# Five and seven raw weight buffers, and gate products with both weight halves in 32 columns

## The chip, the core and the metric

The kernel runs on one core of a Trainium2 chip. The metric is device time in microseconds for one execution. Its engines are TensorE (PE, with its weight loads PEld), VectorE (DVE), ScalarE (ACT), GpSimd (POOL) and SyncE (SP), which here only issues transfers. Each runs its own list of instructions in order; TensorE may load weights for the next product during the present one. On-chip tiles live in named rings of buffers ("tags"): asking for a tile of a tag gives the oldest buffer, and the first write to it waits until its last reader is done.

## The reference

Two layers over 256 context and 256 latent tokens of width 1024: a bidirectional mLSTM, then a latent attention, each followed by a gated feed-forward block with a short convolution. What the change touches is the gate computation of the mLSTM and, beyond that, only how weights are brought in.

```python
x_m = h @ w_up
x_c = jax.nn.silu(_dwconv(x_m, conv_w, conv_b))
...
gates = jnp.einsum("bti,zig->zbgt", x_c, w_gates) + b_gates[:, None, :, None]
li = gates[:, :, :M_HEADS].astype(jnp.float32)
lf = jax.nn.log_sigmoid(gates[:, :, M_HEADS:].astype(jnp.float32))
```

There are two directions z, and in each 4 input gates and 4 forget gates (8 columns g) for every token t; the sum over i has 2048 terms. The gates feed cumulative sums and maxima over the tokens, which weight the mLSTM's attention-like products.

## The kernel before, in words

**Split precision.** Every operand of a large product is held as a high part h, rounded to the product's format, and a low part l = x - h. `mm3` (L311 to L315) forms a product of two such operands from three: h times h, h times l, l times h. The terms low times low are left out.

**The weight stream** (`Stream`, L222 to L282). All weights are packed on the host in one array `ws` of tiles of 128 x 1024 floats (512 KB), in the order of use that `_plan` writes out. For each tile, `_load` issues a transfer on SyncE into a buffer of the tag `raw`, of which there are NRAW = 3. `_split` then casts the raw tile to its high part on ScalarE (L257) and subtracts on VectorE for the low part (L258), into a weight slot of the tag `w` (NB = 3) or, for tiles marked wide, into two buffers of the tag `u` (NU = 31, shared with the activations). A raw buffer is free after the subtraction; after each split, `_split` issues loads until NRAW tiles beyond it are under way. `use(key)` first lets splits run up to AHEAD = 8 tiles further, as far as `limit` and the slots allow. `pump` does the same up to a given tile. Wide tiles are those of the tails of the output products `mout`, `fout0`, `aout` and `fout1`, the attention's first weights (`ukn`, `uv`), and the first four of `fin1`.

**Order of the stages.** `start_up` and `w_up` (up projection and convolution), `w_og` and `w_v` (products of 128-token tiles with moving weights of 512 columns), `gates`, then four heads h of `w_qk`, each of four products j of two weight tiles, with the work of earlier heads in between; then the output product `mout` with its layer norm, the feed-forward products `fin0` and `fout0`, the attention (`dkv`, `ukn`, `uv`, `dq`, `uqr`, `uqn`, scores, `aout`), `fin1`, `fout1` and the last layer norm. In each output product (`outmm`) the last few tiles are held (the tail), so that the first token tile t = 0 finishes all its sums before t = 1 starts. Behind it follow the layer norm's rows (`ln_rows`, L943), the transposes with modulation (`ln_T`, L1003) and the next stage's products. For the layer norm behind `aout`, `build` places the splits of the first `fin1` tiles between the two token tiles' rows: up to QA = 2 before, QB = 4 between, QC = 6 after.

**Work in the background.** Generators are advanced by `tick`: each step runs to the next `yield`. The list `bg` holds such work as the gate chain and the heads' weighting, and `bg2` the modulation weights (`ada_all`, L482), which pass through buffers `ar` (2, loads from `ada_w` on SyncE) and accumulators `acc` (2) on VectorE. The tag `ar` also holds the rotary tables (`rope_load`, L1238), read in the attention before the scores. In the four `w_qk` products of a head, each of the eight weight tiles is followed by two steps of `bg`. The order that stands on each engine at the end is made by a scheduler when the kernel is built, from this order of emission and modelled costs; only the start-up's order is written by hand.

**The gates** (`gates`, L680). The gate weights, 16 columns, are spread on the host over 128 columns: input gates of the two directions at columns 0 and 32, forget gates at 64 and 96. Two weight tiles of 8 blocks hold them; for each of 16 blocks k `mm3` issues three products with 512 moving columns (the activations `xc`, all tokens), 48 in all, into one bank. So the sums come out at partitions 0, 32, 64 and 96, where `gate_chain` (L690) reads them: biases on ScalarE, the logarithm of the sigmoid, scans over tokens on VectorE forwards in partitions 0 to 31 and backwards in 32 to 63, an exponential, two small stores of the result `ad` (read by `head` as broadcasts), and eight transposes into `gcol` (L724 to L730).

Of the kernel before, what the change touches and what calls it, by code (L numbers as in the profile page):

```python
# [7 lines left out]
F32 = mybir.dt.float32  # L8
F32R = mybir.dt.float32r
I32 = mybir.dt.int32  # L10
AF = mybir.ActivationFunctionType
ALU = mybir.AluOpType
AX = mybir.AxisListType

D = 1024
# [14 lines left out]
CW = 1024  # L30

NB, NRAW, NU = 3, 3, 31
# [35 lines left out]
def _plan():  # L68
    ids, order = {}, []

    def add(key, cols, wide=False):
        if key not in ids:
            ids[key] = (len(ids), cols)
        order.append((key, wide))
# [6 lines left out]
    for s in range(4):  # L81
        for c in range(8):
            add(("v", s, c), 1024)
    for c in range(2):
        add(("gates", 0, c), 1024)
    for h in range(H0):
# [35 lines left out]
def _pack(i):  # L122
    ids, _ = _plan()
    ws = np.zeros((len(ids), 128, CW), np.float32)
    wg = i["m_w_gates"][0]
    gz = np.zeros((2 * D, 128), np.float32)
    for z in range(2):
        gz[:, 32 * z:32 * z + 4] = wg[z][:, :4]
        gz[:, 64 + 32 * z:64 + 32 * z + 4] = wg[z][:, 4:]
    ukv = i["a_w_ukv"][0].reshape(256, H1, DN + DV)  # L130
# [8 lines left out]
    for key, (n, cols) in ids.items():  # L139
        kind, a, c = key  # L140
# [4 lines left out]
        elif kind == "gates":  # L145
            b = _stat(gz, 0, 8 * c, 8)
        elif kind == "v":
# [74 lines left out]
class Stream:  # L222


    def __init__(self, k, ids, order, ws):
# [5 lines left out]
        self.raw, self.hl = {}, {}  # L231

    def skip(self, n):
        self.nl = self.ns = self.nu = n

    def _load(self):
        k, j = self.k, self.nl
        n, cols = self.ids[self.order[j][0]]
        t = k.pool.tile([128, CW], F32, tag="raw", name="raw", bufs=NRAW)
        k.nc.sync.dma_start(t[:, :cols], self.ws[n, :, :cols])  # L240
        self.raw[j] = t
        self.nl += 1

    def _split(self):
# [8 lines left out]
        else:  # L253
            w = k.pool.tile([128, 2, CW], F32R, tag="w", name="w", bufs=NB)
            h, l = w[:, 0], w[:, 1]
            self.live.append(j)
        k.nc.scalar.copy(h[:, :cols], raw[:, :cols])  # L257
        k.nc.vector.tensor_sub(l[:, :cols], raw[:, :cols], h[:, :cols])  # L258
        self.hl[j] = (h, l)
        self.ns += 1  # L260
        while self.nl < min(self.ns + NRAW, self.n):
            self._load()
# [22 lines left out]
class K:  # L285
# [393 lines left out]

    def gates(self):  # L680
        gp = self.ps("gates")
        for c in range(2):
            w = self.st.use(("gates", 0, c))
            for kk in range(8):
                k = 8 * c + kk
                cs = slice(kk * 128, (kk + 1) * 128)
                self.mm3(gp, (w[0][:, cs], w[1][:, cs]), (self.xc[k][:, 0], self.xc[k][:, 1]), k == 0, k == 15)
        return gp

    def gate_chain(self, gp):  # L690
        nc = self.nc
        bg = self.smc("bg")
        zi, zf, ab = self.s2("zi"), self.s2("zf"), self.s2("ab")
        R = slice(0, 64)
        nc.scalar.activation(zi[R], gp[0:64], AF.Identity, bias=bg[0:64, 0:1], scale=1.0)
        nc.scalar.activation(zf[R], gp[64:128], AF.Identity, bias=bg[64:128, 0:1], scale=1.0)
# [8 lines left out]
        def scan(o, x, op):  # L705
            nc.vector.tensor_tensor_scan(o[0:32], on[0:32], x[0:32], 0.0, op0=ALU.mult, op1=op)
            nc.vector.tensor_tensor_scan(o[32:64, 0:256][:, ::-1], on[32:64, 0:256], x[32:64, 0:256][:, ::-1],
                                         0.0, op0=ALU.mult, op1=op)
            nc.vector.tensor_tensor_scan(o[32:64, 256:512][:, ::-1], on[32:64, 0:256], x[32:64, 256:512][:, ::-1],
                                         o[32:64, 0:1], op0=ALU.mult, op1=op)  # L710
        scan(B, zf, ALU.add)
        nc.vector.tensor_sub(zi[R], zi[R], B[R])
        yield
        scan(ab, zi, ALU.max)
        nc.vector.tensor_add(B[R], B[R], ab[R])
# [875 lines left out]
```

## Time and profile before

| | us |
|---|---|
| median of 3 runs | 1431.02 |
| lowest and highest run | 1429.1 and 1434.94 |
| the profiled execution | 1429.89 |
| its span (first to last instruction) | 1428.1 |

| engine | busy us | share of the span |
|---|---|---|
| TensorE, products | 1398.6 | 98% |
| TensorE, weight loads | 1176.5 | 82% |
| VectorE | 980.5 | 69% |
| ScalarE | 642.3 | 45% |
| GpSimd | 100.1 | 7% |

The mean granted TensorE clock is 0.996 of full. A row of groups or of the timeline names the line, the engine, the operation, what is written and what is read (out<-in, by the program's names without buffer numbers), and the shape; a bracket at the end of a timeline row gives the engine's idle time before it and what ended it. A wait is written as: who waits, for whom, total us, times, longest. In the chain of waits each piece has a start, a length and a name, and is what set the end at that time. Times count from the span's start.

### The profile page before, as it was taken

How to read it: one execution, taken by the hardware profiler on the slowest of the kernel's cores; microseconds unless marked ns; L12 is line 12 of the kernel's file. 1: busy time of each engine (PE TensorE's matmuls, PEld its weight loads, DVE VectorE, ACT ScalarE, POOL GpSimd, SP SyncE). 2: the span in 40 equal slices, each digit the busy share in tenths (PEclk: the TensorE clock that was granted, in tenths of full speed). 3: DMA queues.
4: the chain of work that ended last, by engine and by line, in shares of the span. 5: the costliest groups of instructions: out<-in, count | busy, mean ns of one | idle time of the engine just before them, and what ended most of it. 6: DMA issues, size and time to landing. Idle time of an engine off the chain costs nothing.

```text
span 1428.1 us, 18819 instructions
## 1 busy us (share of the span) xinstructions
PE 1398.6 (98%) x7095; PEld 1176.5 (82%) x7095; DVE 980.5 (69%) x1437; ACT 642.3 (45%) x972; POOL 100.1 (7%) x185
## 2 busy tenths in 40 slices
PE   7999999999999999999999999999999999899997
PEld 3788888888888888888888888888887998899986
DVE  6696778885775666666787444444567888777755
ACT  6554231224334254464553333334364665555542
POOL 0010110003001010210001000000000001000000
PEclk9999999999999999999999999999999999999999
DMA  9475776777774745555635333335666315367763
GB/s 335 172 240 185 238 250 220 253 232 269 252 230 154 221 136 173 178 178 179 207 129 193 91 116 116 121 123 171 191 187 208 122 53 183 124 187 216 223 198 102
DMA packets 82827, 262.70 MB, mean 184 GB/s; under 512 B 11352, under 2 KB 19752, under 8 KB 82736
## 3 DMA queue, kind: packets, MB, share of 16 engines
q1 hardware_dynamic: 68304, 214.82, 48.2%
q0 software_dynamic: 14144, 46.17, 9.6%
q8 instruction: 55, 0.90, 0.3%
q10 hardware_dynamic: 288, 0.52, 0.1%
q14 instruction: 36, 0.29, 0.1%
HBM read 243.56 MB, written 17.91 MB: 183 GB/s over the span
## 4 chain that ended last, share of the span: by engine, by line
PE 65%; issue 18%; DMA 6%; DVE 6%; ACT 3%; POOL 2%; SPq 0%; DVEq 0%; POOLq 0%; ACTq 0%
PE fin L315 8%; PE fin L313 8%; PE fin L314 8%; PE y L314 5%; PE y L315 5%; PE y L313 5%; PE qk L315 4%; PE qk L313 4%; PE qk L314 4%; DMA raw<-in_ws 3%; DMA ar<-in_ada_w 2%; DVE wu L258 1%; PE up L313 1%; DMA xcr<-xcd 1%; PE up L315 1%
## 5 line engine op out<-in xcount | busy, mean ns | idle before, releaser
L258 DVE TENSOR_TENSOR w<-raw,w 128x1024 fp32r<-128x1024 f32 (+2 forms) x267 | 323.9, 1213 | 240.2 <-ACT w L257 239.7
L257 ACT CAST w<-raw 128x1024 fp32r<-128x1024 f32 (+2 forms) x267 | 278.6, 1045 | 437.2 <-PE tok L315 153.3
L315 PE MATMUL fin<-h,w 128*128 128x256 f32 (+1 forms) x696 | 231.6, 333 | 0.5 <-DVE w L258 0.5
L314 PE MATMUL fin<-h,w 128*128 128x256 f32 (+1 forms) x696 | 231.8, 333 | 0.0
L313 PE MATMUL fin<-h,w 128*128 128x256 f32 (+1 forms) x696 | 231.7, 334 | 0.0
L440 DVE SCALAR_TENSOR_TENSOR acc<-ar,cond,acc 128x1024 f32<-128x1024 f32 x112 | 140.6, 1279 | 36.0 <-DMA ar<-in_ada_w 35.6
L315 PEld LDWEIGHTS fin<-h,w 128*128 128x128 f32 x696 | 132.2, 190 | 13.8 <-DVE w L258 0.9
L314 PEld LDWEIGHTS fin<-h,w 128*128 128x128 f32 x696 | 132.2, 190 | 13.0 <-DVE h L1024 0.2
L313 PEld LDWEIGHTS fin<-h,w 128*128 128x128 f32 x696 | 132.0, 190 | 12.8
L313 PE MATMUL qk<-xc,w 128*128 128x512 f32 x256 | 101.1, 395 | 0.0
L313 PE MATMUL tok<-w,xm 128*128 128x512 f32 x256 | 100.4, 392 | 0.0
L315 PE MATMUL qk<-xc,w 128*128 128x512 f32 x256 | 100.1, 391 | 0.2 <-DVE w L258 0.2
L314 PE MATMUL qk<-xc,w 128*128 128x512 f32 x256 | 99.9, 390 | 0.0
L315 PE MATMUL tok<-w,xm 128*128 128x512 f32 x256 | 99.7, 389 | 0.0
L314 PE MATMUL tok<-w,xm 128*128 128x512 f32 x256 | 99.6, 389 | 0.0
L313 PE MATMUL y<-w,act 128*128 128x512 f32 (+1 forms) x212 | 80.4, 379 | 0.0
L315 PE MATMUL y<-w,act 128*128 128x512 f32 (+1 forms) x212 | 80.1, 378 | 0.0
L314 PE MATMUL y<-w,act 128*128 128x512 f32 (+1 forms) x212 | 80.1, 378 | 0.0
L258 DVE TENSOR_TENSOR wu<-raw,wu 128x1024 fp32r<-128x1024 f32 x36 | 43.9, 1222 | 21.7 <-ACT wu L257 21.3
L315 PEld LDWEIGHTS qk<-xc,w 128*128 128x128 f32 x256 | 48.1, 188 | 10.6 <-DVE w L258 0.6
L313 PEld LDWEIGHTS tok<-w,xm 128*128 128x128 f32 x256 | 48.0, 188 | 10.3
L315 PEld LDWEIGHTS tok<-w,xm 128*128 128x128 f32 x256 | 48.1, 188 | 10.1
(357 smaller groups left out, 2756.6 us busy)
## 6 DMA issues: line engine op xcount, KB each, us to landing
raw<-in_ws SPq DMA_DIRECT2D x300, 512.0 KB, 3.9
ar<-in_ada_w SPq DMA_DIRECT2D x80, 512.0 KB, 4.5
adaw<-in_ada_w SPq DMA_DIRECT2D x32, 256.0 KB, 6.5
xcd<-cv POOLq DMA_DIRECT2D x16, 256.0 KB, 3.2
od<-o POOLq DMA_DIRECT2D x16, 256.0 KB, 4.0
vd<-v POOLq DMA_DIRECT2D x16, 256.0 KB, 3.9
xcr<-xcd POOLq DMA_DIRECT2D x16, 256.0 KB, 6.7
vr<-vd POOLq DMA_DIRECT2D x16, 256.0 KB, 3.8
```

Source lines behind the costliest of these rows:

```text
L257: k.nc.scalar.copy(h[:, :cols], raw[:, :cols])
L258: k.nc.vector.tensor_sub(l[:, :cols], raw[:, :cols], h[:, :cols])
L313: mm(out, w[0], x[0], start=start, stop=False)
L314: mm(out, w[0], x[1], start=False, stop=False)
L315: mm(out, w[1], x[0], start=False, stop=stop)
L440: nc.vector.scalar_tensor_tensor(acc[j], w, s, acc[j], op0=ALU.mult, op1=ALU.add)
```

## The change

It has three parts.

1. **Raw buffers.** The ring into which raw weight tiles are loaded is 3 buffers up to the first tile of `fout0`, then 5 (the two `acc` buffers join), and from the first tile of `aout` on 7 (the two `ar` buffers join as well). After a split, loads are issued as far ahead as the ring has buffers.
2. **Gate products.** The gates' weights are packed as 16 columns a block, 256 columns in all, in one tile of 128 KB instead of two of 512 KB. Their high and low parts are written side by side, 32 columns a block. For each of the 16 blocks two products are issued (with the high and with the low part of the activations), 32 in all, into 32 partitions of a bank. The terms low times low are now among them.
3. **Placing.** `gate_chain` builds a 32 x 128 matrix `sel` from the identity, which adds the high and low columns' sums and puts them at the partitions where they were before; splits the 32 rows of sums into a high and a low part; and after three yields issues two products with `sel`. What follows reads the new bank. The scans yield after each direction, so the chain has 14 yields before its transposes, against 8.

```diff
--- before.py
+++ after.py
@@ -81,8 +81,7 @@
     for s in range(4):
         for c in range(8):
             add(("v", s, c), 1024)
-    for c in range(2):
-        add(("gates", 0, c), 1024)
+    add(("gates", 0, 0), 256)
     for h in range(H0):
         for j in range(4):
             for c in range(2):
@@ -122,11 +121,7 @@
 def _pack(i):
     ids, _ = _plan()
     ws = np.zeros((len(ids), 128, CW), np.float32)
-    wg = i["m_w_gates"][0]
-    gz = np.zeros((2 * D, 128), np.float32)
-    for z in range(2):
-        gz[:, 32 * z:32 * z + 4] = wg[z][:, :4]
-        gz[:, 64 + 32 * z:64 + 32 * z + 4] = wg[z][:, 4:]
+    gz = np.concatenate([i["m_w_gates"][0, 0], i["m_w_gates"][0, 1]], axis=1)
     ukv = i["a_w_ukv"][0].reshape(256, H1, DN + DV)
     uq = i["a_w_uq"][0].reshape(384, H1, DN + DR)
     ukn = np.ascontiguousarray(ukv[:, :, :DN]).reshape(256, H1 * DN)
@@ -143,7 +138,7 @@
         elif kind == "og":
             b = _mov(i["m_w_og"][0][:, a * 512:(a + 1) * 512], 2 * c, 2)
         elif kind == "gates":
-            b = _stat(gz, 0, 8 * c, 8)
+            b = gz.reshape(16, 128, 16).transpose(1, 0, 2).reshape(128, 256)
         elif kind == "v":
             b = _mov(i["m_w_v"][0][:, a * 512:(a + 1) * 512], 2 * c, 2)
         elif kind == "qk":
@@ -230,13 +225,23 @@
         self.limit = self.n
         self.raw, self.hl = {}, {}
 
+        keys = [x[0] for x in order]
+        self.bufs = [(0, [("raw", NRAW)] * NRAW)]
+        self.bufs.append((keys.index(("fout0", 0, 0)), self.bufs[-1][1] + [("acc", 2)] * 2))
+        self.bufs.append((keys.index(("aout", 0, 0)), self.bufs[-1][1] + [("ar", 2)] * 2))
+
+    def ring(self, j):
+        return [x for x in self.bufs if x[0] <= j][-1]
+
     def skip(self, n):
         self.nl = self.ns = self.nu = n
 
     def _load(self):
         k, j = self.k, self.nl
         n, cols = self.ids[self.order[j][0]]
-        t = k.pool.tile([128, CW], F32, tag="raw", name="raw", bufs=NRAW)
+        j0, ring = self.ring(j)
+        tag, bufs = ring[(j - j0) % len(ring)]
+        t = k.pool.tile([128, CW], F32, tag=tag, name="raw", bufs=bufs)
         k.nc.sync.dma_start(t[:, :cols], self.ws[n, :, :cols])
         self.raw[j] = t
         self.nl += 1
@@ -254,11 +259,19 @@
             w = k.pool.tile([128, 2, CW], F32R, tag="w", name="w", bufs=NB)
             h, l = w[:, 0], w[:, 1]
             self.live.append(j)
-        k.nc.scalar.copy(h[:, :cols], raw[:, :cols])
-        k.nc.vector.tensor_sub(l[:, :cols], raw[:, :cols], h[:, :cols])
+        src = raw[:, :cols]
+        if key[0] == "gates":
+
+            v = h[:, 0:512].rearrange("p (k x n) -> p k x n", x=2, n=16)
+            src = src.rearrange("p (k n) -> p k n", n=16)
+            k.nc.scalar.copy(v[:, :, 0], src)
+            k.nc.vector.tensor_sub(v[:, :, 1], src, v[:, :, 0])
+        else:
+            k.nc.scalar.copy(h[:, :cols], src)
+            k.nc.vector.tensor_sub(l[:, :cols], src, h[:, :cols])
         self.hl[j] = (h, l)
         self.ns += 1
-        while self.nl < min(self.ns + NRAW, self.n):
+        while self.nl < min(self.ns + len(self.ring(self.ns)[1]), self.n):
             self._load()
 
     def use(self, key, hold=False):
@@ -678,13 +691,13 @@
         self.xm = None
 
     def gates(self):
+
         gp = self.ps("gates")
-        for c in range(2):
-            w = self.st.use(("gates", 0, c))
-            for kk in range(8):
-                k = 8 * c + kk
-                cs = slice(kk * 128, (kk + 1) * 128)
-                self.mm3(gp, (w[0][:, cs], w[1][:, cs]), (self.xc[k][:, 0], self.xc[k][:, 1]), k == 0, k == 15)
+        w = self.st.use(("gates", 0, 0))[0]
+        for k in range(16):
+            for x in range(2):
+                self.nc.tensor.matmul(gp[0:32], w[:, k * 32:(k + 1) * 32], self.xc[k][:, x],
+                                      start=k == 0 and x == 0, stop=k == 15 and x == 1)
         return gp
 
     def gate_chain(self, gp):
@@ -692,6 +705,22 @@
         bg = self.smc("bg")
         zi, zf, ab = self.s2("zi"), self.s2("zf"), self.s2("ab")
         R = slice(0, 64)
+
+        sel = self.pool.tile([32, 128], F32R, tag="s2", name="sel", bufs=13)
+        nc.vector.memset(sel.bitcast(F32), 0.0)
+        for z in range(2):
+            for f in range(2):
+                i = 8 * z + 4 * f
+                nc.vector.tensor_add(sel[:, 64 * f + 32 * z:64 * f + 32 * z + 4], self.ident[0:32, i:i + 4],
+                                     self.ident[0:32, 16 + i:20 + i])
+        g2 = self.u("g2")
+        self.split(g2[0:32, 0], g2[0:32, 1], gp[0:32])
+        yield
+        yield
+        yield
+        gp = self.ps("gates")
+        for x in range(2):
+            nc.tensor.matmul(gp, sel, g2[0:32, x], start=x == 0, stop=x == 1)
         nc.scalar.activation(zi[R], gp[0:64], AF.Identity, bias=bg[0:64, 0:1], scale=1.0)
         nc.scalar.activation(zf[R], gp[64:128], AF.Identity, bias=bg[64:128, 0:1], scale=1.0)
         nc.vector.scalar_tensor_tensor(ab[R], zf[R], -1.0, zf[R], op0=ALU.mult, op1=ALU.max)
@@ -704,14 +733,15 @@
 
         def scan(o, x, op):
             nc.vector.tensor_tensor_scan(o[0:32], on[0:32], x[0:32], 0.0, op0=ALU.mult, op1=op)
+            yield
             nc.vector.tensor_tensor_scan(o[32:64, 0:256][:, ::-1], on[32:64, 0:256], x[32:64, 0:256][:, ::-1],
                                          0.0, op0=ALU.mult, op1=op)
             nc.vector.tensor_tensor_scan(o[32:64, 256:512][:, ::-1], on[32:64, 0:256], x[32:64, 256:512][:, ::-1],
                                          o[32:64, 0:1], op0=ALU.mult, op1=op)
-        scan(B, zf, ALU.add)
+            yield
+        yield from scan(B, zf, ALU.add)
         nc.vector.tensor_sub(zi[R], zi[R], B[R])
-        yield
-        scan(ab, zi, ALU.max)
+        yield from scan(ab, zi, ALU.max)
         nc.vector.tensor_add(B[R], B[R], ab[R])
         nc.vector.tensor_scalar(ab[R], ab[R], -1.0, None, op0=ALU.mult)
         nc.scalar.activation(B[R], B[R], AF.Exp, scale=-1.0)
```

## Prediction

> **What bounds the kernel now.** I read the page first, then the waits of TensorE, then the timeline around each place where it waits.
>
> ```profile
> span 1428.1 us, 18819 instructions
> PE 1398.6 (98%) x7095; PEld 1176.5 (82%) x7095; DVE 980.5 (69%) x1437; ACT 642.3 (45%) x972; POOL 100.1 (7%) x185
> PE zT L1011 <- DVE z L984: 6.1, 2, 5.0
> PE y L314 <- DVE wu L258: 1.2, 2, 0.8
> ACT wu L257 <- DMA raw<-in_ws: 33.0, 26, 3.2
> ```
>
> TensorE is busy 98% of the span, so only two things can pay: fewer products, or the roughly 30 us in which it is not busy. Of the waits (engine, line, awaited instruction: total us, times, longest) the largest outside the start-up is the transposing product behind a layer norm; waits on weights (line 258) are small. ScalarE, however, waits 33.0 us for raw weights that become wide tiles (wu), and those belong to the tails of the output products, which stand right before the layer norms.
>
> **The gate products.** 48 products go; 32 come, and two placing ones. These rows of the timeline are the first gate product and the first product after the last; the chain's row gives 16 modulation products with a stationary of only 4 columns.
>
> ```profile
> 384.19 0.39 PE L313 MATMUL gates<-xc,w 128*128 128x512 f32 x1
> 395.07 0.39 PE L313 MATMUL qk<-xc,w 128*128 128x512 f32 x1
> 46.20 3.70 PE adar L405 x16
> 384.20:395.00 10.80, 10.80 (x49) 8.97 (x48) 5.87 (x6) 2.69 (x4) 1.34 (x3) 1.00 0.94 347
> ```
>
> 48 products take 395.07 - 384.19 = 10.88 us, 0.227 each: the 0.39 us of a record overlaps its neighbours, and the window (length; busy PE, PEld, DVE, ACT, POOL; clock; DMA share; GB/s) is full. A narrow stationary is shown at 3.70/16 = 0.231 us, so narrowness saves nothing per product; only the count does. 34 at 0.231 are 7.85, at 0.227 they are 7.71: the gain is 3.0 to 3.2 us, and I take **3.1**. End to end records (34 x 0.39 = 13.3) would be a loss of 2.4, but the same record length fits 48 in 10.88, which excludes it.
>
> ScalarE and VectorE work changes little: two weight splits of 1024 columns go, one of 256 columns and one of the 32-row sums come, with a memset and four additions of 4 columns. The narrow operations are not in the trace in this form; the nearest are these.
>
> ```profile
> 389.83 1.06 ACT L257 CAST w<-raw 128x1024 fp32r<-128x1024 f32 x1 [3.90 <-PE gates L315]
> 1177.76 0.37 ACT L318 CAST oT<-o 128x256 fp32r<-128x256 f32 x1
> 410.76 0.59 ACT L318 CAST qk<-qk 128x512 fp32r<-128x512 f32 x1
> 415.28 0.69 DVE L319 TENSOR_TENSOR qk<-qk 128x512 fp32r<-128x512 f32 x1
> 396.57 1.22 DVE L258 TENSOR_TENSOR w<-raw,w 128x1024 fp32r<-128x1024 f32 x1
> 421.70 0.18 DVE L465 SCALAR_TENSOR_TENSOR adav<-adav,adab 64x32 f32<-64x32 f32 x1
> ```
>
> ScalarE: 2 x 1.06 out, 0.37 + 0.59 in, a gain of about 1.1. VectorE: 2 x 1.22 = 2.44 out; in come 0.4 (a third of 1.22), 0.69 and five small operations of at most 0.18, together 2.0. Both are even within a microsecond. The stream loses one 512 KB load and shrinks another to 128 KB on SyncE's queue: 0.92 MB, or 2.6 us at 347 GB/s, in a stage whose DMA share is 0.94. That eases the modulation weights which share the queue; I put it at nothing.
>
> The gate chain gets a detour: split of the sums, the two placing products, and only then the biases. It is a new wait: ScalarE's bias waits for the placing product, behind it on ScalarE stand casts of qk weights, and TensorE waits for those. The chain has 8 yields before its transposes now and 14 after, of 16 steps in the first head's qk products (two per half product of 24 x 0.227 = 5.4 us), so the transposes still fit, moved from the fifth half product to the last. How thin the cover is, these rows show.
>
> ```profile
> 407.12 0.63 ACT L698 ACTIVATE ab<-ab 64x512 f32<-64x512 f32 x1 [8.21 <-DVE ab L697]
> 421.04 0.63 ACT L717 ACTIVATE B<-B 64x512 f32<-64x512 f32 x1 [7.45 <-DVE B L715]
> 417.75 0.50 PE L315 MATMUL qk<-xc,w 128*128 128x512 f32 x1 [0.16 <-DVE w L258]
> ```
>
> ScalarE stood 8.21 and 7.45 us behind the chain, yet TensorE lost only 0.16: three weight slots hide it, with nothing to spare at 417.75. With the chain later and cut finer (a scan per step, 1.2 us at most, where three scans and a subtraction stood in one) I price it at nothing, with bounds of +0.16 gained and, if the cover is gone, the 8.21 + 7.45 = 15.7 lost.
>
> **Five raw buffers, from the first fout0 load.** With three, a load waits for the subtraction three tiles back. Loads keep SyncE's order, and a load into a former ada_w buffer waits for that work's last reader; the last modulation reduction starts at 783.7 us (its row: 141.1 to 783.7), well before the fout0 products.
>
> ```profile
> L447 DVE TENSOR_REDUCE adar<-adat x32: 643/672/686, 141.1 to 783.7; 128x16 f32<-128x512 f32 x32
> 1081.42 1.05 ACT L257 CAST wu<-raw 128x1024 fp32r<-128x1024 f32 x1 [1.92 <-DMA raw<-in_ws]
> 1082.12 0.39 PE L313 MATMUL y<-wu,act 128*128 128x512 f32 x1
> 1085.21 0.49 PE L314 MATMUL y<-wu,act 128*128 128x512 f32 x1 [0.45 <-DVE wu L258]
> 1101.43 0.28 PE L313 MATMUL kn<-ckT,wu 128*128 128x256 f32 x1
> 1163.45 0.87 PE PT L1373 x8
> 1102.45 1.21 DVE L258 TENSOR_TENSOR wu<-raw,wu 128x1024 fp32r<-128x1024 f32 x1
> 1106.67 0.98 PE L1011 MATMUL zT<-ident,z 128*128 128x128 f32 x7 [1.04 <-DVE z L984]
> ```
>
> The fout0 tail is 6 tiles x 4 banks x 3 = 72 products. From 1082.12 to 1101.43 it takes 19.3 us where 72 x 0.227 are 16.3; of the 3.0 over, six transposes among them are 0.65 (8 in 0.87, the row of attention). At most 2.3 is then lost to late weights, one wait of 0.45 among it; the loss may also be switching between kinds of products. I take half, **1.2** (bounds 0 and 2.3). The following layer norm holds the transposes for 1.04; a weight subtraction of 1.21 lies inside it that earlier loads would move ahead. I take half, **0.5** (0 to 1.04).
>
> **Seven raw buffers, from the first aout load.** The last two share space with the rotary tables, whose use ends before attention. Here are the aout tail and the layer norm behind it.
>
> ```profile
> 1206.27 1.05 ACT L257 CAST wu<-raw 128x1024 fp32r<-128x1024 f32 x1 [3.25 <-DMA raw<-in_ws]
> 1215.82 1.05 ACT L257 CAST w<-raw 128x1024 fp32r<-128x1024 f32 x1 [2.48 <-DMA raw<-in_ws]
> 1207.37 0.50 PE L313 MATMUL y<-wu,oT 128*128 128x512 f32 x1 [0.69 <-ACT wu L257]
> 1220.82 0.28 PE L315 MATMUL y<-wu,oT 128*128 128x256 f32 x1
> 1222.80 1.23 DVE L258 TENSOR_TENSOR w<-raw,w 128x1024 fp32r<-128x1024 f32 x1
> 1224.28 1.22 DVE L258 TENSOR_TENSOR w<-raw,w 128x1024 fp32r<-128x1024 f32 x1
> 1227.34 2.82 PE L1011 MATMUL zT<-ident,z 128*128 128x128 f32 x12 [5.01 <-DVE z L984]
> 1221.00:1232.00 11.00, 5.64 (x28) 5.07 (x28) 8.95 (x21) 7.52 (x16) 0.00 (x0) 0.69 0.51 166
> ```
>
> The wait of 0.69 goes with its restart: **0.8** (0 to 0.85). Then 1227.34 - 1220.82 = 6.5 us pass between the last output product and the transposes, and VectorE spends 1.23 + 1.22 of it on splits for the next stage, which came late because the casts before them stood 3.25 and 2.48 us waiting for raw weights. With seven tiles loaded during attention these splits can be over before the last product. I take **2.0** of the 2.45 (bounds 0, if the weight slots and not the loads hold them, and 2.45).
>
> The clock in this window is 0.69. [...]
>
> **The end.** These pieces of the chain show what arrives last in fout1.
>
> ```profile
> 1357.67 0.23 PE y L313
> 1360.45 0.23 PE y L313
> 1399.97 4.30 DMA raw<-in_ws
> 1404.35 1.06 ACT wu L257
> 1405.43 1.24 DVE wu L258
> 1419.81 0.13 PE y L315
> ```
>
> The three-tile cycle is 4.30 + 1.06 + 1.24 = 6.6 us, 2.2 a tile, against 1360.45 - 1357.67 = 2.78 us of products a tile. So the loads barely lead, and the last tiles hold the tail up. 22 x 2.78 = 61.2 from 1357.67 ends at 1418.8; it ended at 1419.9. I take **1.0** (0 to 1.1).
>
> **Sum.** 3.1 + 1.2 + 0.5 + 0.8 + 2.0 + 1.0 = 8.6 us. The profiled execution took 1429.89 (1.8 around its span), so 1421.3; the median of the runs is 1.1 above it, which makes **1422.4**. Its own range: all upper bounds are 3.2 + 2.3 + 1.0 + 0.9 + 2.5 + 1.1 = 11.0 (1420), the gate products with half of the rest about 5.9 (1425), and a shift in the order of the engines' work may move either by 2: 1418 to 1427.
>
> **Rivals.** (1) The deeper ring is hidden anyway: wide tiles and weight slots, not raw buffers, set when a split can start, and ScalarE's 33.0 us only change their name. For it: a cast can also wait for TensorE to free a slot (the 3.90 in the gate rows), and TensorE's own wait for wu is 1.2 us in all. Against: the last tile follows exactly by load, cast and subtraction. Then only 3.1 is left: 1427.9, no change.
>
> (2) Slower: the qk stage of the first head loses its cover. The placing products put a TensorE round trip ahead of ScalarE's chain, the casts behind it come late, and the 8.21 and 7.45 land on TensorE. That costs 15.7 - 8.6 = 7.1: 1438.1. It decides from a stall of 8.6 us on. For it: the 0.16 shows no slack. Against: the sums' split is emitted three steps (8 us) ahead of the products that read it.
>
> (3) The gap behind aout gets so short that the clock stays up in it: the 12 transposes take 2.82 us where 8 take 0.87 at full clock, so 1.3, or 1.5 less.
>
> With all other bounds reached, 11.0 + 1.5 = 12.5: 1418.5. For it: 6.5 - 2.45 leaves 4.1 us, some two thirds of what it is. Against: VectorE and ScalarE still have a whole layer norm to do in it. [...]
>
> **How the numbers follow.** The forecast has 0.48, the hidden ring 0.25, the lost cover 0.10, the kept clock 0.17. The range 1415 to 1431 holds the forecast, the hidden ring and the kept clock with an allowance of 3 to 4 us for their sizes. No change means within 0.5%, 7.2 us, about what a measurement of this kernel can tell: 1423.9 to 1438.2. About 0.7 of the forecast lies below it (0.34), nearly all of the kept clock (0.16) and a little of the hidden ring (0.03): faster 0.53. Slower takes most of the lost cover's upper half and a little for other orders: 0.07. The rest, 0.40, is no change.
>
> **What would show it.** The gate and placing products should take about 7.8 us in all, and the first qk product start 3 us earlier; a wait of TensorE on line 258's successor between 395 and 440 us would be the lost cover. ScalarE's wait of 33.0 for raw wide tiles should shrink to a third; if it does and the waits for z and wu stay, the hidden ring is right. The stretch from the last aout product to the transposes should fall from 6.5 to about 4.5. The forecast is wrong if the span shrinks by under 4 or over 13 us.

## The result and the profile after

The changed kernel takes 1422.28 us (median of 6 runs, 1420.65 to 1426.16) against 1430.68 for the kernel before (6 runs, 1429.1 to 1434.94): a ratio of 0.9936 with a 95% interval of 0.9926 to 0.9947. The forecast was 1422.4, worked out from 1431.02, the median of the first three of those six runs.

The page of the kernel after opens with its span and the engines' busy time (us, share of the span, number of instructions).

```profile
span 1418.5 us, 18778 instructions
PE 1392.4 (98%) x7081; PEld 1170.7 (83%) x7081; DVE 979.2 (69%) x1442; ACT 639.2 (45%) x972; POOL 100.1 (7%) x185
```

The span is 9.6 us shorter. Products were busy 1398.6 us and are busy 1392.4: 6.2 less; the other 3.4 are idle time that went. Lines have moved: `mm3` is now L326 to L328, the cast of a split L270, its subtraction L271, the gate products L699, the placing products L723, the transposes behind a layer norm L1041. The view of waits of the kernel after (who waits, for whom: total us, times, longest):

```profile
PE zT L1041 <- DVE z L1014: 2.6, 1, 2.6
...
PE qk L328 <- DVE w L271: 1.2, 1, 1.2
...
ACT wu L270 <- DMA raw<-in_ws: 9.9, 9, 2.8
...
DVE acc L453 <- DMA ar<-in_ada_w: 39.1, 36, 3.5
```

ScalarE's wait for raw wide tiles fell from 33.0 to 9.9. The transposes' wait behind the layer norms fell from 6.1 to 2.6. The second row was 0.16 us in the kernel before: TensorE now waits 1.2 us for a weight split in the first head's qk stage. The last row, VectorE's wait for modulation weights, is needed further down.

The gate products, in the view of one tile (durations in ns as min/median/max, first and last start, shape), and TensorE's timeline of the kernel after (start, us, engine, line, operation, idle time before it in brackets):

```profile
L699 PEld LDWEIGHTS gates<-xc,w x32: 107/108/112, 383.6 to 390.7; 128*32 128x32 f32 x32
L699 PE MATMUL gates<-xc,w x32: 387/392/398, 383.8 to 391.0; 128*32 128x512 f32 x32
L723 PEld LDWEIGHTS gates<-g,sel x2: 181/182/184, 402.2 to 402.3; 32*128 32x128 f32 x2
```

```profile
383.79 7.56 PE L699 MATMUL gates<-xc,w 128*32 128x512 f32 x32
391.19 0.40 PE L326 MATMUL qk<-xc,w 128*128 128x512 f32 x1
...
401.86 0.39 PE L328 MATMUL qk<-xc,w 128*128 128x512 f32 x1
402.18 0.73 PE L723 MATMUL gates<-g,sel 32*128 32x512 f32 x2
402.83 0.50 PE L326 MATMUL qk<-xc,w 128*128 128x512 f32 x1
...
425.31 0.39 PE L327 MATMUL qk<-xc,w 128*128 128x512 f32 x1
426.90 0.50 PE L328 MATMUL qk<-xc,w 128*128 128x512 f32 x1 [1.20 <-DVE w L271]
427.24 0.39 PE L326 MATMUL qk<-xc,w 128*128 128x512 f32 x1
...
1216.05 0.28 PE L328 MATMUL y<-wu,oT 128*128 128x256 f32 x1
...
1219.42 1.72 PE L1041 MATMUL zT<-ident,z 128*128 128x128 f32 x12 [2.65 <-DVE z L1014]
```

32 products take 391.19 - 383.79 = 7.40 us, 0.231 each, although loading a narrow stationary took 108 ns (the first row above). The two placing products put 402.83 - 401.86 = 0.97 us between two neighbours that are otherwise 0.227 apart: 0.74 for both. The stall at 426.90 lengthens the way from 425.31 to 427.24 to 1.93 us, where two products' pitch is 0.45: 1.48 lost. Behind aout, 1219.42 - 1216.05 = 3.4 us pass between the last product and the transposes, from 6.5.

The span can be cut at the starts of products. The table gives the length of each stage that differs, from TensorE's timeline of both kernels.

| stage | before us | after us | gained |
|---|---|---|---|
| start of the span to the first gate product | 384.2 | 383.8 | 0.4 |
| gates: first gate product to first qk product | 10.9 | 7.4 | 3.5 |
| first head's qk: to its first score product | 45.0 | 47.0 | -2.0 |
| fout0 tail: first wide product to first kn product | 19.3 | 18.5 | 0.8 |
| layer norm and kn: to the last kn product | 37.9 | 37.0 | 0.9 |
| aout: first wide to last product | 22.0 | 21.1 | 1.0 |
| gap: to the last wide fin1 product | 21.4 | 18.2 | 3.1 |
| rest of fin1 | 115.3 | 115.1 | 0.2 |
| fout1: first to last product | 62.1 | 60.9 | 1.2 |

The stages between (heads, mout, fin0, most of fout0, attention) differ by at most 0.1. The end behind the last product differs by 0.3. So the gates brought 3.5 and gave 2.0 back one stage later, and the stages that the prediction named for the ring brought 7.2 with the rest of fin1. The 0.8 of the tail is what was left after a new loss: transposes in it now wait 1.23 us for VectorE, where they waited 0.17. TensorE's timeline of the kernel after:

```profile
1083.71 0.44 PE L1221 MATMUL ckT<-ident,ckr 128*128 128x128 f32 x2 [1.23 <-DVE ckr L1173]
```

### The profile page after: what moved, and what is told of

Read it like the earlier page. It is cut to its first block, busy times and chain, and to the rows that moved or that the text cites. A ratio compares the mean times of both kernels' runs of the same rounds, so it can differ in the third digit from the quotient of the medians.

```text
span 1418.5 us, 18778 instructions
## 1 busy us (share of the span) xinstructions
PE 1392.4 (98%) x7081; PEld 1170.7 (83%) x7081; DVE 979.2 (69%) x1442; ACT 639.2 (45%) x972; POOL 100.1 (7%) x185
## 4 chain that ended last, share of the span: by engine, by line
PE 67%; issue 18%; DMA 5%; DVE 5%; ACT 2%; POOL 2%; SPq 0%; DVEq 0%; POOLq 0%; ACTq 0%
PE fin L326 8%; PE fin L328 8%; PE fin L327 8%; PE y L327 6%; PE y L326 6%; PE y L328 6%; PE qk L328 3%; PE qk L326 3%; PE qk L327 3%; DMA ar<-in_ada_w 2%; DMA raw<-in_ws 2%; PE up L326 1%; PE up L328 1%; PE up L327 1%; DMA xcr<-xcd 1%
## 5 line engine op out<-in xcount | busy, mean ns | idle before, releaser
L271 DVE TENSOR_TENSOR w<-raw,w 128x1024 fp32r<-128x1024 f32 (+2 forms) x265 | 321.4, 1213 | 229.3 <-ACT w L270 228.8
L270 ACT CAST w<-raw 128x1024 fp32r<-128x1024 f32 (+2 forms) x265 | 276.8, 1045 | 428.9 <-PE tok L328 136.8
L328 PE MATMUL fin<-h,w 128*128 128x256 f32 (+1 forms) x696 | 231.5, 333 | 0.5 <-DVE w L271 0.5
L326 PE MATMUL fin<-h,w 128*128 128x256 f32 (+1 forms) x696 | 231.7, 334 | 0.0
L453 DVE SCALAR_TENSOR_TENSOR acc<-ar,cond,acc 128x1024 f32<-128x1024 f32 x112 | 140.5, 1279 | 39.6 <-DMA ar<-in_ada_w 39.1
L328 PEld LDWEIGHTS fin<-h,w 128*128 128x128 f32 x696 | 132.2, 190 | 13.7 <-DVE w L271 0.9
L326 PEld LDWEIGHTS fin<-h,w 128*128 128x128 f32 x696 | 132.1, 190 | 13.1
L328 PE MATMUL qk<-xc,w 128*128 128x512 f32 x256 | 100.2, 391 | 1.2 <-DVE w L271 1.2
L326 PE MATMUL qk<-xc,w 128*128 128x512 f32 x256 | 101.1, 395 | 0.0
L326 PE MATMUL tok<-w,xm 128*128 128x512 f32 x256 | 100.4, 392 | 0.0
L328 PE MATMUL tok<-w,xm 128*128 128x512 f32 x256 | 99.7, 389 | 0.0
L326 PE MATMUL y<-w,act 128*128 128x512 f32 (+1 forms) x212 | 80.4, 379 | 0.0
L328 PE MATMUL y<-w,act 128*128 128x512 f32 (+1 forms) x212 | 80.1, 378 | 0.0
L328 PEld LDWEIGHTS qk<-xc,w 128*128 128x128 f32 x256 | 48.0, 188 | 11.9 <-DVE w L271 2.0
L326 PEld LDWEIGHTS qk<-xc,w 128*128 128x128 f32 x256 | 48.1, 188 | 10.4 <-PE gates L723 0.4
L326 PEld LDWEIGHTS tok<-w,xm 128*128 128x128 f32 x256 | 48.0, 188 | 10.4
L328 PEld LDWEIGHTS tok<-w,xm 128*128 128x128 f32 x256 | 48.0, 188 | 10.1
```

Source lines behind the costliest of these rows:

```text
L270: k.nc.scalar.copy(h[:, :cols], src)
L271: k.nc.vector.tensor_sub(l[:, :cols], src, h[:, :cols])
L326: mm(out, w[0], x[0], start=start, stop=False)
L328: mm(out, w[1], x[0], start=False, stop=stop)
L453: nc.vector.scalar_tensor_tensor(acc[j], w, s, acc[j], op0=ALU.mult, op1=ALU.add)
```

## The experiments

Three questions were open: which part of the change brings what; whether seven buffers do more than five; and whether the stall in the first head's qk stage comes from the change. The table puts all runs together; each is compared with runs of the kernel before that were measured beside it. The stage columns come from one profile of each kernel and add two rows of the table above: gates + qk, tail + kn, aout + gap.

| kernel | median us | before us | ratio, 95% interval | gates + qk | tail + kn | aout + gap |
|---|---|---|---|---|---|---|
| before | | | | 55.9 | 57.2 | 43.4 |
| after | 1422.28 | 1430.68 | 0.9936 (0.9926 to 0.9947) | 54.4 | 55.5 | 39.3 |
| gates_only | 1429.97 | 1433.37 | 0.9985 (0.9975 to 0.9995) | 55.6 | 57.7 | 43.5 |
| rings_only | 1423.76 | 1433.37 | 0.9945 (0.9926 to 0.9964) | 56.8 | 54.9 | 39.8 |
| five_only | 1423.67 | 1433.37 | 0.9949 (0.9931 to 0.9966) | 57.1 | 55.2 | 38.4 |
| seven_only | 1427.37 | 1433.37 | 0.9965 (0.9953 to 0.9977) | 59.1 | 57.0 | 38.1 |
| noada_before | 1430.97 | 1432.46 | 0.9986 (0.9975 to 0.9998) | 55.4 | 60.1 | 43.7 |
| noada_gates | 1426.92 | 1432.46 | 0.9954 (0.9935 to 0.9973) | 52.7 | 57.1 | 43.7 |
| warm | 1421.22 | 1432.46 | 0.9918 (0.9903 to 0.9933) | 54.6 | 55.8 | 38.6 |
| after_poolq | 1427.3 | 1432.46 | 0.9960 (0.9947 to 0.9972) | 59.4 | 55.3 | 40.5 |
| late | 1424.96 | 1431.98 | 0.9944 (0.9930 to 0.9957) | 52.5 | 54.9 | 39.5 |
| late_warm | 1424.74 | 1431.98 | 0.9946 (0.9932 to 0.9960) | 52.5 | 55.3 | 38.3 |
| gates_five | 1422.06 | 1431.98 | 0.9929 (0.9914 to 0.9943) | 55.4 | 54.9 | 40.0 |
| changed_again | 1421.7 | 1431.98 | 0.9929 (0.9915 to 0.9943) | 54.6 | 55.5 | 38.6 |

### One part alone: gates_only, rings_only

gates_only is the changed kernel with three raw buffers throughout; rings_only is the kernel before with the changed ring.

```diff
--- after.py
+++ gates_only.py
-        self.bufs.append((keys.index(("fout0", 0, 0)), self.bufs[-1][1] + [("acc", 2)] * 2))
-        self.bufs.append((keys.index(("aout", 0, 0)), self.bufs[-1][1] + [("ar", 2)] * 2))
```

> The gate products and the placing as in the changed kernel, three raw buffers throughout. Theory (the gain of the gate products is partly given back in the first head's qk stage): 1.5 to 2.2 us faster than before, about 1428.6; the stretch from the first qk product to the first score product of head 0 is near 47.0 us as in the changed kernel (45.0 before), with one wait of TensorE of about 1.2 us on a weight subtraction in it; everything after head 0 keeps its length. Rival (the stall is made by the deeper ring or is chance): 3.1 us faster, 1427.5, and the stretch is 45.0 to 45.6 us.

> The gates as before, five and then seven raw buffers. Theory (the two parts act in different stages and add up): 7.3 us faster, about 1423.4, with the gap from the last aout product to the twelve transposes at 3.4 us (6.5 before). Rival (the parts help each other by shifting the schedule): under 5 us faster.

The ring alone gives 0.55% and the gates alone 0.15%; both together gave 0.64% and, in changed_again, 0.71%. The parts add up within their intervals, and most of the gain is the ring. gates_only leaves tail + kn and aout + gap about as they were before (57.7 and 43.5); rings_only has them about as after (54.9 and 39.8). The qk stage of gates_only took 48.2 us, so the stall is there without the deeper ring; its size is taken up below. In rings_only the way from the last aout product to the twelve transposes took 4.4 us, not the 3.4 that was expected.

### Five or seven: five_only, seven_only, gates_five

five_only keeps five buffers from fout0 to the end; seven_only keeps three up to aout and then takes all seven; gates_five is the changed kernel without the third ring.

```diff
--- rings_only.py
+++ five_only.py
-        self.bufs.append((keys.index(("aout", 0, 0)), self.bufs[-1][1] + [("ar", 2)] * 2))
```

```diff
--- rings_only.py
+++ seven_only.py
-        self.bufs.append((keys.index(("fout0", 0, 0)), self.bufs[-1][1] + [("acc", 2)] * 2))
-        self.bufs.append((keys.index(("aout", 0, 0)), self.bufs[-1][1] + [("ar", 2)] * 2))
+        self.bufs.append((keys.index(("aout", 0, 0)), self.bufs[-1][1] + [("acc", 2)] * 2 + [("ar", 2)] * 2))
```

> The gates as before, five raw buffers from the first fout0 tile to the end. If five are enough for the aout and fout1 tails too (a cycle of 4.4 + 1.05 + 1.24 = 6.7 us over five tiles is 1.3 us a tile, below the 2.2 of three and below the products' 2.8): as fast as five and seven, 7 us faster. If the two further buffers carry the aout stage: only the 1.6 us of the fout0 tail and the layer norm behind it, plus 1.1 of fout1, so 2.7 us faster.

> The gates as before, three raw buffers up to the first aout tile, seven from there. If the stages are independent: 7.3 less 1.6, so 5.7 us faster, the fout0 tail and the stretch to the last kn product as long as before (19.3 and 37.9 us). If the gap behind aout depends on how early the weights before aout arrived: under 4 us faster.

> The changed kernel with five raw buffers kept to the end instead of seven. If the two further buffers are not needed: within 0.1% of the changed kernel, the gap behind aout and the fout1 stage as long as there (18.2 and 61.1 us). If they are: 2 us or more slower, with the gap nearer to 21.

five_only takes as long as rings_only, and gates_five as long as changed_again beside it (the same ratio, 0.9929). With five buffers to the end, aout took 21.0 us and fout1 60.9 in both kernels, as with seven (21.1 and 60.9). seven_only has the gain behind aout (38.1) but not the one in tail + kn (57.0). Its TensorE timeline shows the old wait still there behind fout0, and another one of which more is said below:

```profile
421.25 0.50 PE L324 MATMUL qk<-xc,w 128*128 128x512 f32 x1 [2.59 <-DVE w L267]
...
1109.80 0.98 PE L1020 MATMUL zT<-ident,z 128*128 128x128 f32 x7 [1.04 <-DVE z L993]
```

The wait of 1.04 is that of the kernel before, to the hundredth; the timelines of five_only and of the changed kernel have no wait of these transposes there. So buffers 4 and 5 do the whole work and the two that come from the rotary tables add nothing that these runs can tell.

### The stall in the first head's qk stage: noada_before, noada_gates

Up to the start of fin0 the kernels before, rings_only, five_only and seven_only issue the same instructions in the same order on every engine. Still their qk stage took 45.0, 46.0, 46.2 and 48.3 us. What differs is how long TensorE waits for a weight split: 0.16 us in the kernel before, 2.59 in seven_only (the row above). VectorE's timeline of the kernel after shows what the split stands behind:

```profile
399.19 1.28 DVE L453 SCALAR_TENSOR_TENSOR acc<-ar,cond,acc 128x1024 f32<-128x1024 f32 x1 [3.27 <-DMA ar<-in_ada_w]
...
404.59 1.28 DVE L453 SCALAR_TENSOR_TENSOR acc<-ar,cond,acc 128x1024 f32<-128x1024 f32 x1 [1.19 <-DMA ar<-in_ada_w]
...
408.24 1.28 DVE L453 SCALAR_TENSOR_TENSOR acc<-ar,cond,acc 128x1024 f32<-128x1024 f32 x1 [1.23 <-DMA ar<-in_ada_w]
410.36 1.28 DVE L453 SCALAR_TENSOR_TENSOR acc<-ar,cond,acc 128x1024 f32<-128x1024 f32 x1 [0.83 <-DMA ar<-in_ada_w]
...
424.59 0.53 DVE L746 TENSOR_SCALAR ab<-ab 64x512 f32<-64x512 f32 x1
425.04 0.67 DVE L332 TENSOR_TENSOR qk<-qk 128x512 fp32r<-128x512 f32 x1
425.64 2.34 DVE L271 TENSOR_TENSOR w<-raw,w 128x1024 fp32r<-128x1024 f32 x2
```

Four accumulations of modulation weights wait 3.27 + 1.19 + 1.23 + 0.83 = 6.5 us for their loads; the gate chain's scans come late behind them, and the split that TensorE wants at 425.5 (425.31 + 0.23) starts at 425.64. The four kernels with the same order show the link by themselves. Counted from the first qk product, the last accumulation ahead of that split starts at 16.3 us in the kernel before, 17.3 in rings_only, 17.5 in five_only and 19.6 in seven_only; TensorE's wait is 0.16, 1.13, 1.38 and 2.59. Here is that accumulation in the kernel before, then in seven_only:

```profile
411.38 1.27 DVE L440 SCALAR_TENSOR_TENSOR acc<-ar,cond,acc 128x1024 f32<-128x1024 f32 x1
```

```profile
414.87 1.28 DVE L449 SCALAR_TENSOR_TENSOR acc<-ar,cond,acc 128x1024 f32<-128x1024 f32 x1 [0.91 <-DMA ar<-in_ada_w]
```

If late accumulations are the cause, the stall must go when they go, with old and new gates alike.

```diff
--- before.py
+++ noada_before.py
+            if nconds == 1 and k > 0:
+                yield
+                continue
```

noada_gates is gates_only with the same three lines.

> The kernel before, without seven eighths of the modulation sums of the second layer's last four vectors (28 loads of 512 KB and 28 accumulations on VectorE are left out). Theory (head 0's qk stage is stretched by VectorE standing in its order behind accumulations whose loads are late, by an amount that changes from run to run: 45.0 to 48.3 us in profiles of kernels with the same order there): the stretch from the first qk product to the first score product is 44.5 us or less, no wait of TensorE on a weight in it, and the kernel is 0.5 to 3 us faster than before. Rival (the gate chain's scans alone make the wait): the wait stays, and the time is within 0.1% of before.

> The new gate products with three raw buffers, and the same 28 loads and accumulations left out. Theory: the stretch is that of the kernel without them plus the two placing products, 0.5 us, and gates and stretch together are 3.1 us shorter than in it; the kernel is 3.1 us faster than that one. Rival (the detour of the gate chain itself holds up casts and with them TensorE): a wait of over 1 us stays in the stretch, and the kernel is under 2 us faster than that one.

In neither of the two does TensorE's timeline show any wait between the first gate product and the end of that stage. Here is VectorE's timeline of noada_gates; the end of the chain and the two splits of the last fence come at 418.37 and 419.31, about 6.3 us earlier:

```profile
418.37 0.42 DVE L747 TENSOR_SCALAR ab<-ab 64x512 f32<-64x512 f32 x1
418.71 0.68 DVE L330 TENSOR_TENSOR qk<-qk 128x512 fp32r<-128x512 f32 x1
419.31 2.55 DVE L269 TENSOR_TENSOR w<-raw,w 128x1024 fp32r<-128x1024 f32 x2
```

The qk stage took 44.6 us in noada_before and 45.3 in noada_gates: the 0.7 between them are the two placing products. These two kernels leave out VectorE's work (1.28 us an accumulation) together with the waiting for loads, so they can't tell one from the other; the four profiles with the same work above can. Gates and qk together differ by 55.43 - 52.68 = 2.75 us. This is what the gate change is worth where nothing stalls. The medians of the two differ by 4.05, but other stages differ as well: tail + kn is 3.0 us longer in the profile of noada_before (60.1 against 57.1), where single weight loads of kn took up to 335 ns, and at most 192 in noada_gates. With the loads in place, the five profiles with new gates whose background work is unchanged (after, gates_only, warm, gates_five, changed_again) have a mean of 54.9 us, the four with old ones (before, rings_only, five_only, seven_only) 57.2: 2.3 less. The excess over the stage without stalls is thus about as large with old gates (57.2 - 55.4 = 1.8 us) as with new (54.9 - 52.7 = 2.2). It was there before, in a size that changes from one execution to the next; the profile on which the prediction rests happened to show a small one. The detour has a small wait of its own in three of the five: the second placing product waits for the split of the sums, which stands on VectorE behind the same accumulations, 0.67 us in gates_only (the row below), 0.39 in warm and 0.13 in gates_five.

```profile
403.64 0.49 PE L721 MATMUL gates<-g,sel 32*128 32x512 f32 x1 [0.67 <-DVE g L330]
```

### Getting rid of it: after_poolq, late

If the loads are late because they stand on SyncE's queue behind weight loads, another queue would help. after_poolq issues the 32 loads for single vectors of modulation on GpSimd's queue.

```diff
--- after.py
+++ after_poolq.py
-            nc.sync.dma_start(w, self.a["ada_w"][l, k * 128:(k + 1) * 128, c * D:(c + 1) * D])
+            (nc.gpsimd if nconds == 1 else nc.sync).dma_start(w, self.a["ada_w"][l, k * 128:(k + 1) * 128, c * D:(c + 1) * D])
```

> The changed kernel with the 32 modulation loads of the second layer's last four vectors on GpSimd's queue instead of SyncE's. If the late weights in head 0's qk stage come from raw loads standing behind these loads in SyncE's order: the wait of 1.2 us goes and the kernel is 1 to 2 us faster than the changed one. If they come from VectorE standing behind the accumulations: the wait stays, and the time is within 1 us of the changed one.

Neither branch came true: the wait stayed, but the kernel became 5 us slower than the changed one, and the stage grew to 52.0 us. Its view of waits:

```profile
PE qk L328 <- DVE w L271: 4.1, 3, 2.1
...
DVE acc L453 <- DMA ar<-in_ada_w: 45.6, 35, 4.0
```

VectorE waits longer for these loads (45.6 us against 39.1 in the changed kernel), and TensorE 4.1 us instead of 1.2. So taking them out of SyncE's order did not make them come earlier; what makes them late was not settled. Part of the longer stage is the clock: behind a wait of 2.06 us, TensorE ran 3.41 us at half clock, which is 1.7 us of work lost (half of 3.41, an estimate). The view by stretches of time (length; busy PE, PEld, DVE, ACT, POOL with numbers of instructions; granted clock; DMA share; GB/s):

```profile
401.32:404.73 3.41, 3.41 (x10) 2.64 (x9) 2.33 (x2) 0.00 (x0) 0.54 (x1) 0.50 0.79 275
```

late takes the modulation's steps out of the first head's qk stage and leaves them to later stages.

```diff
--- after.py
+++ late.py
-ADA_T, ADA_Q = 1.25, 0.75
+ADA_T, ADA_Q = 1.0, 0.75
...
-                self.tick(nt, ADA_Q)
+                self.tick(nt, ADA_Q if h else 0)
```

> The changed kernel with the modulation's background steps at 1.0 instead of 1.25 per weight tile of the og and v products and none in head 0's qk products, so that no accumulation stands on VectorE between the gate products and head 1; all of the work is still done, more of it in fin0. If these accumulations stretch head 0's qk stage: its length falls from 47.0 to about 45.3 us (what the kernel without them has), no wait of TensorE on a weight in it, and the kernel is 1 to 3 us faster than the changed one. If other work on VectorE only takes their place: 46.5 to 48 us again, and the same time.

The stage is clean, 45.1 us, 1.9 less than after, and yet the kernel takes 1424.96 where changed_again, measured beside it, takes 1421.7. The four heads behind the stage grew from 181.0 to 186.2. In them stands a new wait of TensorE, the longest of this row in the view of waits, and behind it 3.41 us at half clock. The view of waits, TensorE's and VectorE's timeline, and a stretch:

```profile
PE hnT L955 <- DVE oh L949: 5.3, 2, 3.6
```

```profile
568.53 0.44 PE L955 MATMUL hnT<-ident,oh 128*128 128x128 f32 x2 [3.63 <-DVE oh L949]
```

```profile
566.79 1.28 DVE L453 SCALAR_TENSOR_TENSOR acc<-ar,cond,acc 128x1024 f32<-128x1024 f32 x1
568.00 1.67 DVE L949 TENSOR_SCALAR oh<-oh,ss 128x512 f32<-128x512 f32 x4
```

```profile
569.86:573.25 3.39, 3.39 (x11) 2.72 (x11) 3.31 (x8) 1.26 (x2) 0.00 (x0) 0.50 0.63 209
```

The wait of 3.6 us and the 1.7 lost to the half clock make the 5.2; the other wait of the row, 1.7 us at 646.67, lies behind the heads and stands in changed_again too (1.7). VectorE got the moved work at a place where TensorE waits for it, too. Both attempts failed: the stall could not be removed with a few lines.

### The clock behind aout: warm, late_warm, changed_again

The third rival of the prediction was that the clock stays up in the gap. In the profile after it doesn't, as the view by stretches of time shows: the clock falls after the transposes have begun.

```profile
1219.00:1220.00 1.00, 0.58 (x5) 0.58 (x6) 0.37 (x1) 0.81 (x1) 0.00 (x0) 1.00 0.47 193
1220.00:1221.00 1.00, 1.00 (x9) 0.74 (x7) 0.40 (x1) 0.99 (x3) 0.00 (x0) 0.81 0.00 0
1221.00:1222.00 1.00, 0.77 (x4) 0.63 (x4) 1.00 (x4) 1.00 (x5) 0.00 (x0) 0.50 0.00 0
```

warm and late_warm add 24 products of 128 columns behind the last aout product, which nothing reads; the placing of them is the same in both.

```diff
--- after.py
+++ warm.py
+        idle = k.ps("idle")
+        for _ in range(24):
+            nc.tensor.transpose(idle[:, 0:128], k.ident, k.ident)
         k.drain()
```

> The changed kernel with 24 products of 128 columns that nobody reads, placed behind the last aout product (24 x 0.109 = 2.6 us, the length of TensorE's idle time there). If the half clock after the gap (1220.3 to 1224.0 us, about 3.5 us at 0.5) costs time: the next products run at full clock, and the kernel is 1.0 to 1.8 us faster than the changed one, 1420.8. If the products at half clock are held up by the layer norm's own results anyway: no faster, and up to 1 us slower where the extra products end after the layer norm.

> The same, and the 24 idle products behind the last aout product. If both gains stand and are independent: 0.7 to 1.2 us faster than the kernel with the later modulation alone, and 2 to 4 us faster than the changed one.

> The changed kernel itself, for comparison on the same chip: 1422 to 1423 us where the kernel before takes 1431 to 1432. Theory (the length of head 0's qk stage changes from run to run with the loads' times): 46 to 49 us in this profile, the gate products 7.4 and the stages from fin0 on within 0.7 us of the first profile.

In warm the clock stays at 1.00 and the gap takes 17.5 us. But in changed_again, the same kernel as after, the clock stayed at 1.00 as well, without idle products and after a longer idle time than in after. TensorE's timeline of changed_again, then those of five_only and gates_five:

```profile
1217.94 0.28 PE L328 MATMUL y<-wu,oT 128*128 128x256 f32 x1
...
1221.84 1.53 PE L1041 MATMUL zT<-ident,z 128*128 128x128 f32 x12 [3.18 <-DVE z L1014]
```

```profile
1224.11 1.53 PE L1020 MATMUL zT<-ident,z 128*128 128x128 f32 x12 [2.51 <-DVE z L993]
```

```profile
1219.30 0.28 PE L327 MATMUL y<-wu,oT 128*128 128x256 f32 x1
...
1223.84 2.82 PE L1040 MATMUL zT<-ident,z 128*128 128x128 f32 x12 [2.51 <-DVE z L1013]
```

The twelve transposes took 1.53 us in one and 2.82 in the other, and the idle time just before them was 2.51 us in both; the stretch 1224 to 1225 has a clock of 1.00 in five_only and of 0.50 in gates_five. These two gaps are not quite alike: four earlier transposes stand in them, and gates_five had idled 0.87 us more around those, five_only 0.26. The pair after and changed_again has no such difference, and there the longer idle time (3.18 against 2.65) kept the clock.

How much TensorE worked around the gap is shown by the same view, first for the 3.41 us ahead of the half clock in after and for the half clock itself, then for two stretches of 3.41 us and three of 1 us in changed_again:

```profile
1217.21:1220.62 3.41, 1.20 (x11) 1.20 (x12) 1.71 (x7) 1.72 (x4) 0.00 (x0) 1.00 0.60 163
1220.64:1224.03 3.39, 3.16 (x15) 2.76 (x14) 3.39 (x9) 3.39 (x11) 0.00 (x0) 0.50 0.02 5
```

```profile
1216.83:1220.24 3.41, 1.83 (x16) 1.59 (x14) 3.34 (x7) 1.09 (x2) 0.00 (x0) 1.00 0.72 231
1220.24:1223.65 3.41, 1.53 (x12) 1.29 (x12) 1.74 (x7) 2.33 (x6) 0.00 (x0) 1.00 0.39 135
...
1219.00:1220.00 1.00, 0.00 (x0) 0.00 (x0) 0.93 (x4) 0.00 (x0) 0.00 (x0) 1.00 0.82 193
1220.00:1221.00 1.00, 0.00 (x0) 0.00 (x0) 0.60 (x3) 0.30 (x1) 0.00 (x0) 1.00 0.64 168
1221.00:1222.00 1.00, 0.16 (x1) 0.16 (x2) 0.76 (x3) 0.58 (x1) 0.00 (x0) 1.00 0.69 279
```

In after most of the 2.65 us of idle time lies in the stretch ahead of the half clock: TensorE was busy for 1.20 of its 3.41 us, and the next 3.39 had a clock of 0.50. In changed_again it was busy for 1.83 and 1.53 us of the two stretches, and the clock stayed at 1.00. But that comparison hangs on where the stretches are laid: from 1219 to 1222 TensorE was busy for 0.16 of 3 us in changed_again, and the clock stayed at 1.00 there too. What decides whether the clock falls was not shown.

Of the eight profiles with a deep ring behind aout and no idle products, the clock held in three (five_only, seven_only, changed_again: gaps of 17.4, 17.1 and 17.6) and dropped in five (after, rings_only, gates_five, late, after_poolq: 18.2, 18.7, 18.9, 18.5 and 19.5). The clock is worth some 18.8 - 17.4 = 1.4 us by these means, and it can't be resolved in the total time: the interval of warm overlaps those of after and changed_again, and late_warm is as fast as late, not 0.7 to 1.2 us faster as expected. For the rest, changed_again came as expected (qk 47.2 us), with a median a little under the range given.

No run is clearly faster than the changed kernel. gates_five equals it with less.

## Why the prediction was right, step by step

The forecast of 1422.4 met 1422.28, and its sum of 8.6 us met a difference of medians of 8.4. But the sum came out by errors of both signs: the gates were put too high and the ring too low. That it met the medians to 0.2 us is luck; that the gain comes from the stages named is not.

**Gate products: the mechanism was right, the size was not.** The count alone pays: 32 products at 0.231 us, as forecast, in spite of the narrower weight load. The two placing products took 0.74 instead of 0.46, so the term is 10.88 - 7.40 - 0.74 = 2.7, not 3.1. Then the step "I price it at nothing", for the cover of the gate chain, failed in this profile: 1.48 us were lost at 426.90, within its bounds (+0.16 to -15.7). The experiments showed that this stall isn't made by the detour. It is the old one of 0.16, which the prediction took as a fixed property of the kernel and which lies between 0.16 and 2.6 us in executions with the same order. On average the change is worth 2.3 us here, and 2.75 without the stall. The prediction also called its cover thin with "nothing to spare", and then priced that at nothing; the bounds, not the price, were what the rows allowed.

**Five raw buffers.** The fout0 tail gave 0.8 (forecast 1.2) and the layer norm with kn 0.9 (0.5): 1.7 together, as summed. The wait of 1.04 at the transposes went away, all of it, twice the 0.5 taken. The tail's 0.8 hides a loss: without the new wait for VectorE (1.23 us, 0.17 before) it would have given about 1.9, an estimate from 0.8 and these two waits.

**Seven raw buffers: the stages were right, the cause was named too narrowly.** aout gave 1.0 (forecast 0.8), the gap 3.1 (2.0), fout1 1.2 (1.0). But five_only and gates_five show that two more buffers than three are enough for all of them. The prediction worked out 2.2 us for a tile of the three-buffer cycle (6.6 / 3) and did not ask what five would make of it: 1.3 by the same working (6.6 / 5), half of the 2.78 that the products of a tile take. By this working a sixth and seventh have nothing left to hide, and no run shows a gain from them.

**The gap was undersized.** From the last aout product to the transposes the forecast was 4.5 us; it was 3.4 in after, 3.9 in changed_again and 4.5 in gates_five (rows above: 1219.42 - 1216.05, 1221.84 - 1217.94, 1223.84 - 1219.30). In after that is 3.15 gained, more than the 2.45 set as the upper bound. The bound counted only the two splits that stood inside the gap. The splits ahead of it had held VectorE back as well: the layer norm's first row for the second token tile starts 1.28 us before the last aout product in the kernel before and 4.62 us before it in after (at 1219.54 and 1211.43 in VectorE's timelines).

**The rivals.** That the ring is hidden anyway falls with rings_only (0.9945). The lost cover was real in kind and some 1.5 us in size, not 15.7; it didn't need the change. The clock stayed up in three of eight profiles, worth 1.4 us, close to the 1.5 that was worked out. The rival's condition did not hold: the length of the gap was to decide, and of two profiles of the same kernel the one with the longer idle time kept the clock (3.18 us in changed_again against 2.65 in after). So it is not a case of its own: the changed kernel showed both, and what decides was not shown.

## What to carry to other kernels

Where a loader's cycle (load, cast, subtract) divided by its buffers comes near the time that the products of one tile take, two more buffers paid here in every place where the stream restarts; work out the cycle for each number of buffers before finding space for more. A single profile doesn't tell how thin a cover is: a wait of 0.16 us behind an engine that stands in order behind late transfers can be 2.6 in the next execution, so before a stall is charged to a change, look at the same stage in kernels whose order there is unchanged. Moving background work off a tight stage only helps if the engine that does it has room where it lands. And a wait of TensorE can cost more than its length: half clock followed the wait of 2.06 us in after_poolq, for 3.41 us, and that of 3.63 in late, for 3.39, about 1.7 us more in each.

## What was not expected of the hardware

**The clock.** It fell to 0.50 after an idle time of 2.65 us in after, and stayed at 1.00 after 3.18 in changed_again. So the idle time just before the transposes did not decide between these two. TensorE had been busy for 1.20 of the 3.41 us ahead of the half clock in after; in changed_again it was busy for 0.16 of the 3 us from 1219 to 1222, at a clock of 1.00 (the rows above). The experiments do not show what decides.

**Narrow weight loads.** A stationary of 32 columns loads in 108 ns, where one of 128 columns (and 32 rows) took 181 to 184 for the placing products (the rows of the gates' tile above). The products still start 0.231 us apart, so the shorter load isn't seen.
